# One decoder layer on one core: the first products' order, the norm of x on the way out of its transpose, eight early groups, and a ring of their own for gate rows

## The chip, the core and the metric

One NeuronCore of a Trainium2 chip runs the whole kernel. Its engines have a queue each: PE (TensorE, matrix products; its weight loads are shown as PEld), DVE (VectorE), ACT (ScalarE), POOL (GpSimd) and SP (SyncE, which here only issues DMAs). The metric is the device time of one execution in microseconds, and less is better. Of the kernel before there are three timed runs, and a trace of one more, profiled execution.

## The reference

```python
shift, scale, gate = split(silu(c) @ w_ada + b_ada, 3)
h = rms_norm(x, norm_pre_w) * (1 + scale) + shift
proj = h @ w_in        # q k v a b z of the delta net; qk v i f o z of the mLSTM; g_A g_B
y_A = (rms_norm(gated_delta_rule(...)) * silu(gdn_z)) @ w_proj_gdn
y_B = (sigmoid(ml_o) * rms_norm(mlstm(...)) * silu(ml_z)) @ w_proj_mlstm
out = (sigmoid(g_A) * y_A + sigmoid(g_B) * y_B) @ w_out
x + gate * rms_norm(out, norm_post_w)
```

x has 256 rows (SEQ) and 2048 columns (D), all in float32; c is one vector, so silu(c) @ w_ada is one row of 3 × 2048 numbers. The execution reads 354.40 MB from HBM, nearly all of it weights, each read once.

## The kernel before

**Products.** Each float32 operand is split in a high part (`whi`, `h_hi`; a cast on ACT, L169) and a remainder (`wlo`, `h_lo`; a subtraction on DVE or POOL, L170), and each product is made as three: hi·hi, hi·lo and lo·hi (`mm3`, L221 to L223). Weights come as units of up to 1 MB (`raw`, three buffers) that are used in pieces of 1024 columns; whi and wlo have four buffers each. `share` (L172) decides which remainders go to POOL instead of DVE: it counts up by 0.8 per column until POOL gets one, from a start of −3072.

**Order.** Nothing is scheduled by a compiler: each engine's queue holds instructions in the order in which the program writes them. `Stream` takes units; `_loads` issues a unit's DMAs on SP as soon as the unit that used its buffer before (one ring of buffers per name) is prepared in program order, and stops at the first unit for which that doesn't hold. `prep` (cast and remainder, or a sum) runs up to `ahead` pieces before `use` (the products). After each used piece `Side.step` lets every side generator go one `yield` further; norms, recurrences and gates are written as such generators, and `wait(n)` is n steps.

**Start.** silu(c) is spread over all partitions by products with one row (`csil`, L282). x is squared, and `rs` = 1/rms comes from DVE and POOL. `x_scale` (L300) multiplies x by rs on ACT, two chunks of 128 columns at a time; `x_turn` (L304) transposes them on PE, and ACT copies them back. Each row of w_ada (1 MB, `ar`, three buffers) is multiplied by csil and summed on DVE (L355); two rows give shift and scale of a chunk k of h. `h_chunk(k)` (L327) then makes sh, s1, hf, h_hi on ACT and h_lo on DVE for k < 2 and else on POOL. The 14 start groups are those columns of w_in that need h first: `BLOCKS` (L340) says which groups take which chunks in which order, and how many w_ada rows are loaded ahead. In block 0 the first `NE` = 6 groups take chunk 0, then the others chunks 0 and 1. Sums that aren't complete are kept in SBUF tiles `part` (L411 to L415).

**After the start** come eight periods of the delta net (`base_inverse`, L712, inverts triangles on DVE: `xx` goes to DRAM as `xd`, and comes back as `xcmp`, which DVE transposes into `ycmp` for PE), four mLSTM stages, in which 16 rows of w_ada for the gate are read as well (`add_gate_unit`, L1073, summed on DVE into `gacc`, L1089, and loaded into the ring of weights), and the output products.

Of the kernel before, what the change touches and what calls it, by code (L numbers as in the profile page):

```python
# [117 lines left out]
def hybrid_layer_kernel(  # L118
# [53 lines left out]
    share = [-3072.0, START_SHARE]  # L172
# [56 lines left out]
    ct = const("ct", c_t, [P, KC])  # L229
    sil = cp.tile([P, KC], F32, name="sil")  # L230
    A.activation(sil, ct, AF.Silu)
# [39 lines left out]
    crow = [part[4 + i].rearrange("p b c -> p (b c)")[0:1] for i in range(2)]  # L271
    for i in range(2):
        SP.dma_start(crow[i], c_row[:, i * 1024:(i + 1) * 1024])
    for b in range(2):
        SP.dma_start(xs[:, b], x[b * P:(b + 1) * P])
    SP.dma_start(ident, consts[:, 0:128])
    bat = const("bat", b_ada_t, [P, 32])
    npre = const("npre", npre_t, [P, KC])
    for i in range(2):
        A.activation(crow[i], crow[i], AF.Silu)  # L280
    for q in range(4):
        T.matmul(csil[:, q * 512:(q + 1) * 512], one_row, crow[q // 2][:, (q % 2) * 512:(q % 2 + 1) * 512],  # L282
                 start=True, stop=True)
    late_c = {}

    def late_consts():
        SP.dma_start(con[:, 128:512], consts[:, 128:512])
        late_c.update(gcv=const("gcv", gconv, [P, 256]), mcv=const("mcv", mconv, [P, 64]),
# [3 lines left out]
    for b in range(2):  # L292
        A.activation(part[2].rearrange("p b c -> p (b c)"), xs[:, b, 0:1024], AF.Square, accum_out=ss[:, b, 0:1])
        V.scalar_tensor_tensor(part[3].rearrange("p b c -> p (b c)"), xs[:, b, 1024:D], 1.0, xs[:, b, 1024:D],
                               op0=ALU.mult, op1=ALU.mult, accum_out=ss[:, b, 1:2])
    V.tensor_reduce(rs, ss, axis=AX.X, op=ALU.add)
    V.tensor_scalar(rs, rs, 1.0 / D, EPS, op0=ALU.mult, op1=ALU.add)
    pow_(rs, rs, mhalf[:, 0:2])

    def x_scale(k):  # L300
        for b in range(2):
            A.activation(xs[:, b, k * P:(k + 2) * P], xs[:, b, k * P:(k + 2) * P], AF.Copy, scale=rs[:, b:b + 1])

    def x_turn(k):  # L304
        ps = jtile("xps")
# [4 lines left out]
        A.copy(xs[:, :, k * P:(k + 2) * P], ps.rearrange("p (b c) -> p b c", b=2))  # L310


    for k in range(0, 8, 2):
        x_scale(k)
        if k in (2, 4):
            x_turn(k - 2)
# [3 lines left out]
    V.scalar_tensor_tensor(bnp, bat[:, KC:2 * KC], 1.0, npre, op0=ALU.add, op1=ALU.mult)  # L320

    def load_ada(src):
        raw = sp.tile([P, 2048], F32, name="ar", tag="ar", bufs=ADA_BUFS)
        SP.dma_start(raw, src)
        return raw

    def h_chunk(k):  # L327

        A.activation(sh[:, k:k + 1], ad[:, k:k + 1], AF.Identity, bias=bat[:, k:k + 1])
        A.activation(s1[:, k:k + 1], ad[:, KC + k:KC + k + 1], AF.Identity, bias=bnp[:, k:k + 1],  # L330
                     scale=npre[:, k:k + 1])
        hf = sp.tile([P, S], F32, name="hf", tag="hf", bufs=2)
        A.activation(hf.rearrange("p (b t) -> p b t", b=2), xs[:, :, k * P:(k + 1) * P], AF.Identity, bias=sh[:, k:k + 1], scale=s1[:, k:k + 1])
# [15 lines left out]
    def ada_units():  # L349

        adders = []
        for k in range(KC):
            for pt in range(2):
                def prep(h, raw, k=k, pt=pt):
                    V.scalar_tensor_tensor(raw, raw, 1.0, csil, op0=ALU.mult, op1=ALU.mult,  # L355
                                           accum_out=ad[:, pt * KC + k:pt * KC + k + 1])
                    j = 2 * (2 * k + pt) - 4
                    if 4 <= j < 16:
                        x_turn(j)
                        if j < 12:  # L360
                            x_scale(j + 4)
# [1044 lines left out]
```

## Time and profile before

| | |
|---|---|
| timed runs | 1602.19, 1605.75, 1607.46 us (median 1605.75) |
| the profiled execution | 1603.88 us, of it a span of 1601.9 us |
| mean granted clock | 0.999 |
| instructions | 25461 |
| DMA | 372.37 MB, 232 GB/s in the mean |

All times of the trace count from the start of the span. A matmul's duration overlaps the next one's, so the distance of two starts tells the rate. "Idle before" is the time that an engine did nothing ahead of an instruction, and the name behind the arrow is what ended it. The other lines of the profile stand where the prediction uses them.

### The profile page before, as it was taken

The page shows a single profiled execution, that of the slowest core. Times are in us where ns is not written, and L with a number is a line of the kernel's source. Part 1 is how long each engine was busy: PE and PEld are TensorE (multiplying, and loading weights), DVE is VectorE, ACT ScalarE, POOL GpSimd, SP SyncE. Part 2 cuts the span into 40 slices and gives each one's busy share as a digit, 9 for nine tenths or more (in the row PEclk, how much of TensorE's full clock was granted, in tenths as well). Part 3 has the DMA queues.
Part 4 walks back from the last instruction along what each step waited for, and adds up shares of the span by engine and source line. Part 5 has one row for each costly group of instructions (what it writes and reads, how often), then busy time and mean ns, then how long its engine had stood idle before and what let it go on. Part 6 is the DMA issues. An engine that isn't in the chain of part 4 may idle for free.

```text
span 1601.9 us, 25461 instructions
## 1 busy us (share of the span) xinstructions
PE 1577.8 (98%) x9844; PEld 1388.1 (87%) x9844; DVE 1150.1 (72%) x1801; ACT 941.0 (59%) x1503; POOL 236.7 (15%) x193
## 2 busy tenths in 40 slices
PE   7999999999999999999999999999999999999998
PEld 4888888899999999999999999889988888888886
DVE  6695556765689788887888788776878556756654
ACT  7754446765656575757576666655565644444443
POOL 1787771000000010000000000000000000100100
PEclk9999999999999999999999999999999999999999
DMA  9898775965565646564656465566888667766573
GB/s 375 339 406 335 279 274 195 289 238 191 170 203 175 205 148 204 164 193 169 193 169 195 149 197 176 187 214 247 290 308 305 227 249 284 283 246 244 200 273 113
DMA packets 96261, 372.37 MB, mean 232 GB/s; under 512 B 26262, under 2 KB 46214, under 8 KB 58252
## 3 DMA queue, kind: packets, MB, share of 16 engines
q1 hardware_dynamic: 96140, 370.75, 66.2%
q8 instruction: 77, 1.26, 0.3%
q14 instruction: 44, 0.36, 0.1%
HBM read 354.40 MB, written 16.31 MB: 231 GB/s over the span
## 4 chain that ended last, share of the span: by engine, by line
PE 79%; issue 13%; DMA 3%; DVE 2%; ACT 2%; POOL 1%; SPq 0%; DVEq 0%; POOLq 0%; ACTq 0%
PE pn L223 35%; PE pt L223 28%; PE py L223 8%; DMA raw<-in_dram 1%; POOL mg L1196 1%; PE psa L223 1%; ACT whi L169 1%; DVE wlo L170 1%; DMA ya<-o_dr 1%; DMA ar<-in_dram 1%; PE mz L816 0%; PE mq L807 0%; PE pa L828 0%; PE po L856 0%; PE po L857 0%
## 5 line engine op out<-in xcount | busy, mean ns | idle before, releaser
L170 DVE TENSOR_TENSOR wlo<-raw,whi 128x1024 fp32r<-128x1024 f32 x454 | 561.5, 1245 | 253.9 <-ACT whi L169 248.8
L169 ACT CAST whi<-raw 128x1024 fp32r<-128x1024 f32 (+1 forms) x517 | 533.0, 1046 | 327.1 <-PE pn L223 148.1
L223 PE MATMUL pt<-h_hi,whi 128*128 128x256 f32 x1280 | 367.8, 287 | 0.0
L223 PE MATMUL pt<-h_hi,wlo 128*128 128x256 f32 x1280 | 362.0, 283 | 0.0
L223 PE MATMUL pt<-h_lo,whi 128*128 128x256 f32 x1280 | 362.0, 283 | 0.0
L223 PE MATMUL pn<-whi,h_hi 128*128 128x512 f32 x896 | 353.9, 395 | 6.6 <-ACT whi L169 5.7
L223 PE MATMUL pn<-wlo,h_hi 128*128 128x512 f32 x896 | 350.0, 391 | 1.1 <-POOL wlo L170 0.6
L223 PE MATMUL pn<-whi,h_lo 128*128 128x512 f32 x896 | 349.8, 390 | 0.0
L223 PEld LDWEIGHTS pt<-h_hi,whi 128*128 128x128 f32 x1280 | 245.3, 192 | 1.4
L223 PEld LDWEIGHTS pt<-h_lo,whi 128*128 128x128 f32 x1280 | 245.4, 192 | 0.3
L223 PEld LDWEIGHTS pt<-h_hi,wlo 128*128 128x128 f32 x1280 | 245.2, 192 | 0.0
L223 PEld LDWEIGHTS pn<-whi,h_hi 128*128 128x128 f32 x896 | 168.8, 188 | 42.5 <-ACT whi L169 6.1
L223 PEld LDWEIGHTS pn<-wlo,h_hi 128*128 128x128 f32 x896 | 168.8, 188 | 36.0 <-DVE wlo L170 1.3
L223 PEld LDWEIGHTS pn<-whi,h_lo 128*128 128x128 f32 x896 | 168.6, 188 | 35.3
L170 POOL TENSOR_TENSOR wlo<-raw,whi 128x1024 fp32r<-128x1024 f32 (+1 forms) x63 | 146.3, 2332 | 67.1 <-ACT whi L169 64.9
L223 PE MATMUL py<-whi,yhi 128*128 128x512 f32 x384 | 150.6, 392 | 0.7 <-ACT vt L1017 0.7
L223 PE MATMUL py<-whi,ylo 128*128 128x512 f32 x384 | 149.6, 390 | 0.0
L223 PE MATMUL py<-wlo,yhi 128*128 128x512 f32 x384 | 149.4, 389 | 0.0
L411 DVE TENSOR_TENSOR part<-pn,part 128x512 f32<-128x512 f32 x112 | 73.7, 685 | 52.6 <-PE pn L223 52.6
L169 ACT CAST yhi<-ya 128x512 fp32r<-128x512 f32 x48 | 29.9, 622 | 130.9 <-PE py L223 127.4
L170 DVE TENSOR_TENSOR ylo<-ya,yhi 128x512 fp32r<-128x512 f32 x48 | 33.2, 692 | 86.7 <-ACT yhi L169 78.7
L593 DVE SCALAR_TENSOR_TENSOR qs<-pt,gcv,qs 128x255 f32<-128x255 f32 (+2 forms) x192 | 92.2, 480 | 4.6
(251 smaller groups left out, 1790.8 us busy)
## 6 DMA issues: line engine op xcount, KB each, us to landing
raw<-in_dram SPq DMA_DIRECT2D x259, 1024.0 KB
ar<-in_dram SPq DMA_DIRECT2D x32, 1024.0 KB
raw<-in_dram SPq DMA_DIRECT2D x16, 512.0 KB
ya<-o_dr SPq DMA_DIRECT2D x32, 256.0 KB
gate_dr<-part SPq DMA_DIRECT2D x11, 512.0 KB
gb<-rows SPq DMA_DIRECT2D x20, 256.0 KB
raw<-in_dram SPq DMA_DIRECT2D x6, 768.0 KB
ug<-ud SPq DMA_DIRECT2D x32, 128.0 KB
```

The lines of the kernel that those rows point to most:

```text
L169: A.copy(hi, src)
L170: (eng or V).tensor_tensor(lo, src, hi.bitcast(F32), op=ALU.subtract)
L223: T.matmul(ps, l, r, start=start and i == 0, stop=stop and i == 2, skip_group_check=True)
L411: V.tensor_tensor(part[g][:, b], ps[b], part[g][:, b], op=ALU.add)
L593: V.scalar_tensor_tensor(dst[:, n, sh:], src[:, 0:S - sh], taps(n, 3 - sh), dst[:, n, sh:], op0=ALU.mult, op1=ALU.add)
L1196: G.tensor_tensor(mcols(b, hf, cg), mcols(b, hf, cg), s_, op=ALU.add)
```

## The change

At the start the row of c is loaded by ACT's queue, w_ada's first row ahead of x by SP's, its second in two halves, and three small constants by POOL's; silu(c) by partitions is made later. A tile of zeros is multiplied with itself four times (`keep_busy`) after csil, and once more behind the first transposes. Squares, rs, the two sums, the first cast (now on DVE) and the first chunk are written out in one function, `first_chunk`, which scales only the first two chunks of x; hf is read from PSUM. The first twelve products go by part over four banks (`use_first`). For the other chunks raw x is transposed, and DVE multiplies it with `rsb`, rows of rs, on the way out of PSUM (`x_norm`). rsb comes from two POOL operations and two products with the identity, written after the eighth group of block 0 (`rs_rows`). sh and s1 of the other chunks are DVE's; h_lo is DVE's for chunks 1 and 15, else POOL's. Eight groups are early instead of six, and share starts at −1024. In the periods of the delta net a step is moved ahead of `block_rows` and into `base_inverse`, and xd's store, its reload and the transpose are two steps apart each. A gate row is loaded as four tiles of 512 columns, in a ring of one row.

```diff
-    share = [-3072.0, START_SHARE]
+    share = [-1024.0, START_SHARE]
+    begin = []
...
+        if begin:
+            begin.pop()(raw[:, 0:n], hi, lo)
+            return hi, lo
...
+    crow = ada_tile()[0:1]
+    A.dma_start(crow, c_row)
+    ar0, ar1 = load_ada(w_ada[0]), ada_tile()
     for b in range(2):
         SP.dma_start(xs[:, b], x[b * P:(b + 1) * P])
...
+    for t, src in ((bat, b_ada_t), (npre, npre_t), (ident, consts[:, 0:128])):
+        G.dma_start(t, src)
     for i in range(2):
+        SP.dma_start(ar1[:, i * 1024:(i + 1) * 1024], w_ada[1][:, i * 1024:(i + 1) * 1024])
...
+    zero = part[-1][:, 0]
+    G.memset(zero, 0.0)
+    zps = jtile("zps")
+    def keep_busy(n):
+        for _ in range(n):
+            T.matmul(zps, zero[:, 0:P], zero, start=True, stop=True)
...
+    def x_norm(k):
+        ps = x_turn(k)
+        V.tensor_tensor(xs[:, :, k * P:(k + 2) * P].rearrange("p b (k t) -> p b k t", k=2), ps,
+                        rsb.rearrange("p (b t) -> p b t", b=2).unsqueeze(2).broadcast_to([P, 2, 2, P]), op=ALU.mult)
+    def rs_rows():
+        ps = jtile("rsp")
+        for b in range(2):
+            rc = part[-1][:, 1, b * P:(b + 1) * P]
+            G.tensor_scalar(rc, zero[:, 0:P], rs[:, b:b + 1], None, op0=ALU.add)
+            T.matmul(ps[:, b * P:(b + 1) * P], rc, ident, start=True, stop=True)
+        A.copy(rsb, ps[:, 0:S])
...
+    def first_chunk(src, hi, lo):
+        keep_busy(4)
+        half = [slice(i * 1024, (i + 1) * 1024) for i in range(2)]
...
+        G.tensor_tensor(rs, ss[:, :, 0], ss[:, :, 1], op=ALU.add)
+        G.tensor_scalar(rs, rs, 1.0 / D, EPS, op0=ALU.mult, op1=ALU.add)
+        pow_(rs, rs, mhalf[:, 0:2])
+        ada_sum(ar0, slice(0, D), ad[:, 0:1])
+        V.scalar_tensor_tensor(bnp, bat[:, KC:2 * KC], 1.0, npre, op0=ALU.add, op1=ALU.mult)
+        for i in range(2):
+            ada_sum(ar1, half[i], adh[:, i:i + 1])
...
+        A.activation(sh[:, 0:1], ad[:, 0:1], AF.Identity, bias=bat[:, 0:1])
+        V.tensor_copy(hi, src)
+        for b in range(2):
+            A.activation(xs[:, b, 0:2 * P], xs[:, b, 0:2 * P], AF.Copy, scale=rs[:, b:b + 1])
+        xps = x_turn(0)
+        keep_busy(1)
+        V.tensor_tensor(lo, src, hi.bitcast(F32), op=ALU.subtract)
+        hf = sp.tile([P, S], F32, name="hf", tag="hf", bufs=2)
+        A.activation(hf.rearrange("p (b t) -> p b t", b=2), xps[:, :, 0], AF.Identity, bias=sh[:, 0:1],
+                     scale=s1[:, 0:1])
+        split(hf, h_hi[:, 0], h_lo[:, 0], V)
...
-        split(hf, h_hi[:, k], h_lo[:, k], V if k < 2 else G)
+        split(hf, h_hi[:, k], h_lo[:, k], V if k in (1, KC - 1) else G)
...
-    NG, NE = len(START), 6
+    NG, NE = len(START), 8
...
-    BLOCKS = ((EARLY, 0, 1, 1.1, 3.5), (REST, 0, 2, 4, 8), (EARLY, 1, 3, 8, 12), (REST, 2, 2, 12, 16.5),
+    BLOCKS = ((EARLY, 0, 1, 1.1, 2.8), (REST, 0, 2, 4, 8), (EARLY, 1, 3, 8, 13), (REST, 2, 2, 13, 16.5),
...
+                    if pt:
+                        V.scalar_tensor_tensor(s1[:, k:k + 1], ad[:, KC + k:KC + k + 1], npre[:, k:k + 1],
+                                               bnp[:, k:k + 1], op0=ALU.mult, op1=ALU.add)
+                    else:
+                        V.tensor_tensor(sh[:, k:k + 1], ad[:, k:k + 1], bat[:, k:k + 1], op=ALU.add)
+                    if 2 <= k < 9 and pt == 0:
+                        x_norm(2 * k - 2)
...
+        def use_first(hi, lo):
+            pss = [[jtile(f"pn{i}") for i in range(2)] for _ in range(2)]
+            for i, (l, r) in enumerate(((h_hi, hi), (h_hi, lo), (h_lo, hi))):
+                for g in range(2):
+                    for b in range(2):
+                        T.matmul(pss[g][b], l[:, 0, b * P:(b + 1) * P], r[:, g * 512:(g + 1) * 512],
+                                 start=i == 0, stop=i == 2, skip_group_check=True)
...
+                stream.ahead = 3 if bi else 2
+                if bi == 0 and g == 0:
+                    use_first(hi, lo)
+                    return
...
+                    if bi == 0 and gg == NE - 1:
+                        rs_rows()
-                stream.ahead = 3 if bi else 1
...
-        yield from wait(4)
+        yield from wait(3)
...
-        yield from wait(1)
+        yield from wait(2)
         SP.dma_start(xd.rearrange("qq q rg m i -> (q rg m) qq i"), xx)
+        yield from wait(2)
...
-        yield from wait(5)
+        yield from wait(2)
...
+        raw = [yp.tile([P, 512], F32, name=f"graw{q}", tag=("yhi", "ylo")[q % 2], bufs=2) for q in range(4)]
+        for q in range(4):
+            SP.dma_start(raw[q], src[:, q * 512:(q + 1) * 512])
...
-        stream.add(w_ada[32 + i], prep, None, 1)
+        stream.add(w_ada[32 + i], prep, None, 1, load=(load_gate, "gate", 1))
```

What this does to the queues, as the two programs write them (line, operation, out and in by their names, size, and how many in a row). PE from its first product of csil up to the first products of w_in, before:

```order
L282 MATMUL csil<-part_110,one_row 128x512 x2
L282 MATMUL csil<-part_111,one_row 128x512 x2
L308 MATMUL xps<-con,xs 128x128 x8
L223 MATMUL pn_221<-whi,h_hi 128x512
L223 MATMUL pn_221<-wlo,h_hi 128x512
L223 MATMUL pn_221<-whi,h_lo 128x512
L223 MATMUL pn_222<-whi,h_hi 128x512
```

and the same place of PE's queue after the change (zps is the bank of the zeros, part_117 the tile that holds them, con the constants with the identity):

```order
L297 MATMUL csil<-ar,one_row 128x512 x4
L305 MATMUL zps<-part_117 128x512 x4
L329 MATMUL xps<-con,xs 128x128 x4
L305 MATMUL zps<-part_117 128x512
L476 MATMUL pn_212<-whi,h_hi 128x512
L476 MATMUL pn_213<-whi,h_hi 128x512
L476 MATMUL pn_214<-whi,h_hi 128x512
L476 MATMUL pn_215<-whi,h_hi 128x512
L476 MATMUL pn_212<-wlo,h_hi 128x512
```

Five products of zeros stand around the first transposes, of which there are four instead of eight, and the first four products need whi and h_hi alone.

POOL's queue from the loads of the small constants to the first of its remainders, after the change (rsx is rs, ssx the sums of squares; before, the queue had only the power and then remainders):

```order
L291 DMA bat<-in_dram 128x32
L291 DMA npre<-in_dram 128x16
L291 DMA con<-in_dram 128x128
L299 MEMSET part_117 128x512
L369 TENSOR_TENSOR rsx<-ssx 128x2
L370 TENSOR_SCALAR rsx<-rsx 128x2
L223 TENSOR_TENSOR rsx<-rsx,mhalf 128x2
L170 TENSOR_TENSOR wlo<-raw,whi 128x1024 x3
L344 TENSOR_SCALAR part_117<-part_117,rsx 128x128 x2
L170 TENSOR_TENSOR wlo<-raw,whi 128x1024
```

The two operations for rows of rs stand behind three remainders on POOL, and the products that read them stand on PE behind the 48th product of w_in.

SP's queue around the last store of xd, which falls into the first mLSTM stage, before:

```order
L164 DMA raw<-in_dram 128x2048 x7
L745 DMA xd<-xx 128x8x32
L748 DMA xcmp<-xd 32x1x256 x4
L164 DMA raw<-in_dram 128x2048 x5
L901 DMA o_dr<-oT 128x2x256 x2
```

and after (graw are the tiles of the gate rows):

```order
L164 DMA raw<-in_dram 128x2048 x2
L824 DMA xd<-xx 128x8x32
L828 DMA xcmp<-xd 32x1x256 x4
L1157 DMA graw_11234<-in_dram 128x512
L1157 DMA graw_11235<-in_dram 128x512
L1157 DMA graw_11236<-in_dram 128x512
L1157 DMA graw_11237<-in_dram 128x512
L164 DMA raw<-in_dram 128x2048
L981 DMA o_dr<-oT 128x2x256 x2
```

Gate rows are no longer among the raw loads, and four DMAs stand in SP's queue for one of them.

More of the change, by code (lines that the diff above doesn't have):

```diff
@@ L290, in late_consts @@
                       gnw=const("gnw", gnorm, [P, 1]), mnw=const("mnw", mnorm_t, [P, KC]))
[L292 to L302, printed above, removed]
+    rsb = con[:, 128:384]
     def x_turn(k):
@@ L309, in x_turn @@
                             ident)
[L310 to L316, printed above, removed]
-    bnp = sp.tile([P, KC], F32, name="bnp")
[L320 to L325, printed above, removed]
+        return ps.rearrange("p (b k t) -> p b k t", b=2, k=2)
@@ L351, in ada_units @@
         adders = []
-        for k in range(KC):
+        for k in range(1, KC):
             for pt in range(2):
@@ L541, in hybrid_layer_kernel @@
             ahead = first + (last - first) * j / len(fs)
-            while ia < len(ada) and ia < ahead:
-                ada[ia]()
+            while ia - 2 < len(ada) and ia < ahead:
+                ada[ia - 2]()
                 ia += 1
@@ L694, in gdn_stage1 @@
                 scored[0] = p
+        yield
         block_rows(res, z)
-        yield
         for blk in range(2):
@@ L712, in base_inverse @@
     def base_inverse(zg, res, zr):
+        yield
         ud = res["ud"]
```

79 lines of the change are left out of this document (49 added, 30 removed).

## The prediction

> **What bounds the kernel now.** First the page's totals, then busy time cut into stages by the windows view (columns: busy us and count of each engine, granted clock, DMA share, GB/s).
>
> ```profile
> PE 1577.8 (98%) x9844; PEld 1388.1 (87%) x9844; DVE 1150.1 (72%) x1801; ACT 941.0 (59%) x1503; POOL 236.7 (15%) x193
> ...
> 0.00:20.00 20.00, 9.16 (x16) 3.82 (x16) 8.27 (x18) 12.74 (x24) 0.92 (x5) 1.00 0.86 338
> 20.00:86.00 66.00, 64.00 (x278) 50.95 (x279) 48.33 (x48) 51.76 (x90) 39.58 (x22) 1.00 0.94 368
> 86.00:257.00 171.00, 171.00 (x756) 141.57 (x755) 109.91 (x126) 78.33 (x96) 115.88 (x55) 1.00 0.83 310
> ...
> 1063.00:1100.00 37.00, 34.60 (x319) 31.37 (x318) 24.78 (x40) 21.81 (x43) 1.85 (x1) 1.00 0.70 256
> ...
> 1585.00:1602.00 17.00, 9.24 (x41) 7.32 (x39) 6.39 (x11) 2.76 (x6) 3.68 (x4) 0.90 0.34 123
> ```
>
> TensorE is the bound: 1577.8 of 1601.9 us, 24.1 us idle. So the change can win only in the idle time and in the slow matmuls of the start: 10.8 us before the first product at 20.00, 2.0 us up to 86, 2.4 us at 1063 to 1100, and 7.8 us at the end, which it doesn't touch. From 86 to 1063 nearly every microsecond is PE's, so what is won at 86 is kept, and what isn't won by 86 is lost.
>
> Then the timeline of the start (start, duration, engine, line; in brackets what ended the idle time).
>
> ```profile
> 1.82 0.83 SPq L275 DMA_DIRECT2D xs<-in_dram  x2
> ...
> 3.88 7.19 PE L282 MATMUL csil<-part,one_row 1*128 1x512 f32 x8 [3.88 <-ACT part L280]
> 6.68 1.06 ACT L293 ACTIVATE part<-xs 128x1024 f32<-128x1024 f32 x1 [1.91 <-DMA xs<-in_dram]
> 9.26 1.06 ACT L293 ACTIVATE part<-xs 128x1024 f32<-128x1024 f32 x1 [1.43 <-DMA xs<-in_dram]
> 11.06 0.71 POOL L219 TENSOR_TENSOR rsx<-rsx,mhalf 128x2 f32<-128x2 f32 x1 [10.62 <-DVE bnp L320]
> ...
> 15.22 2.29 DVE L355 SCALAR_TENSOR_TENSOR ar<-ar,csil 128x2048 f32<-128x2048 f32 x1
> 17.55 0.39 ACT L330 ACTIVATE s<-ad,bnp,npre 128x1 f32<-128x1 f32 x1 [1.12 <-DVE ar L355]
> 17.97 0.60 ACT L333 ACTIVATE hf<-xs,sh,s 128x256 f32<-128x256 f32 x1
> 18.60 0.40 ACT L169 CAST h_hi<-hf 128x256 fp32r<-128x256 f32 x1
> 18.91 1.99 ACT L169 CAST whi<-raw 128x1024 fp32r<-128x1024 f32 x2
> 20.00 0.80 PE L223 MATMUL pn<-whi,h_hi 128*128 128x512 f32 x1 [5.67 <-ACT whi L169]
> 21.27 0.79 PE L223 MATMUL pn<-wlo,h_hi 128*128 128x512 f32 x1 [0.47 <-DVE wlo L170]
> ...
> 22.29 0.63 PE L223 MATMUL pn<-whi,h_hi 128*128 128x512 f32 x1
> ...
> 24.42 0.63 PE L223 MATMUL pn<-whi,h_lo 128*128 128x512 f32 x1
> ...
> 25.59 0.39 PE L223 MATMUL pn<-whi,h_hi 128*128 128x512 f32 x1
> ...
> 29.44 0.39 PE L223 MATMUL pn<-whi,h_lo 128*128 128x512 f32 x1
> ...
> 34.12 1.04 PE L308 MATMUL xps<-con,xs 128*128 128x128 f32 x8
> ...
> 36.02 0.50 PE L223 MATMUL pn<-wlo,h_hi 128*128 128x512 f32 x1 [0.63 <-POOL wlo L170]
> ```
>
> Read backwards, the chain is: w_ada's second row summed (15.22), scale, `hf`, `h_hi`, the weight's cast, the first product. From 22.29 to 24.42 five products start 0.427 us apart, from 25.59 to 29.44 seventeen 0.226 apart. So the array is at half rate for 4.8 us after 20.00, although the clock column says 1.00.
>
> **The change, part by part.**
>
> *Loads.* Today x is issued at 1.82 and its first half used at 6.68: 4.86 later; the second follows 2.58 later. With ar0 first on SP (at about 0.7), I estimate ar0 at 5.5, x at 8.2 and 10.8, ar1's halves at 12.1 and 13.4: the second w_ada row 1.8 earlier than 15.22, now half at a time.
>
> *csil* keeps its 7.19 us and ends near 10.6, so DVE sums ar0 from 10.6 to 12.9, `bnp`, and then two halves of about 1.2 each; s1 is there at about 16.0.
>
> *The norm* has three squares on ACT after 8.2: 10.8 + 2 × 1.2 = 13.2. Then POOL's add, scale and pow: an add on POOL takes 0.35 by the row below, pow 0.71, so about 14.7; two ACT scales (0.46 each, L302) give 15.6.
>
> *The zeros.* One fp32 product of 512 columns takes 7.19 / 4 = 1.80 us in csil's row, or 0.95 at the fast rate (by 0.226 / 0.427). Four take 3.8 to 7.2 us; I take 5.7, half slow and half fast: 10.6 to 16.3. The transposes wait behind them on PE (0.6 us for four), then `hf` 0.60, `h_hi` 0.40: first product at **18.05** instead of 20.00. The fifth, 0.95, runs beside `hf`; slow, it would cost 0.7. The weight's cast moves from ACT to DVE behind s1 (about 1.2, by 1.22 of DVE's row of this size below; done near 17.2), the remainder takes 1.22 more, so wlo (18.4) and h_lo (18.9) come before products 5 and 9 want them (19.0, 19.9): the order by part is what hides them. If the zeros worked, twelve products take 12 × 0.227 = 2.7, done at 20.8 instead of 25.59: **4.8 us**.
>
> ```profile
> L640 POOL TENSOR_TENSOR b<-gb,ngt 128x2 f32<-128x2 f32 x16 | 5.7, 354 | 0.0
> L302 ACT ACTIVATE xs<-xs,rsx 128x256 f32<-128x256 f32 x16 | 7.3, 516 | 1.4 <-POOL rsx L219 1.4
> ...
> L411 DVE TENSOR_TENSOR part<-pn,part 128x512 f32<-128x512 f32 x112 | 73.7, 685 | 52.6 <-PE pn L223 52.6
> L170 POOL TENSOR_TENSOR wlo<-raw,whi 128x1024 fp32r<-128x1024 f32 x58 | 139.7, 2415 | 66.5 <-ACT whi L169 64.3 <-PE pn L223 2.2
> ```
>
> The array's rate is where a rule can be held against a row. csil kept PE busy for 7.19 us with one-row operands and the transposes after 12.37 and the products from 20.00 still ran slow. The Trainium skill, "TensorE: Matmul & The Clock Gate", Part 1, says that about 3.4 us of sustained work opens the clock and an idle window of that length closes it again, by how busy the array is. By that rule the zeros open it, and the fifth one after the transposes keeps it open, which is the sum above; by csil's row they may not, which is rival A. No run here shows full-height zeros.
>
> *What takes part of it back.* Eight groups first means 48 products before the next chunk: 18.05 + 48 × 0.227 = 28.9, while DMA is full (0.94 of the window 20 to 86 already). Loads start only 1.1 us earlier than now, so PE will catch up with them, and with four banks copied out at once: I give 1 to 2 us (bounds 0 and 4.8, all of it). Then two new matmuls (`rsp`) on PE wait for two POOL operations that stand behind POOL's wlo pieces, 2.4 us each. I estimate them at 31.3 to 32.6, when PE could have been there at 29.5 to 30.5: about 2 us of stall. The 49th product comes at 32.5 to 33.8 (today after the transposes of 34.12, at 34.91).
>
> *x's new way out* spares ACT two scales (1.03) and a copy per pair of chunks and gives DVE one operation from PSUM (near L411's 0.69), and sh and s1 too. ACT and DVE have 14 and 18 us to spare in the window 20 to 86, so this is worth nothing directly. One more set of four transposes falls behind the first product: 0.5 (half of 34.12's 1.04). Against that, stalls such as the 0.63 at 36.02 mostly go, POOL starting earlier and more groups being open: 1.5 of the 2.0 idle us. At 86 I count 1.8 + 1.5 − 0.5 = **2.8 us** gained (0.3 to 5.5).
>
> *GDN waits and gate rows.* At 1063 to 1100:
>
> ```profile
> PE mp L781 <- DVE ycmp L752: 1.9, 1, 1.9
> ...
> PE pab L223 <- POOL h_lo L170: 0.4, 1, 0.4
> ...
> SPq L164 <- DVE gacc L1089: 34.1, 15, 4.2
> SPq L748 <- DMA xd<-xx: 24.1, 8, 6.2
> 1065.75 1.29 DVE gacc L1089
> 1067.05 5.00 DMA raw<-in_dram
> ...
> 1072.13 1.06 ACT whi L169
> ...
> 1073.22 1.22 DVE wlo L170
> ...
> 1087.45 8.72 DMA raw<-in_dram
> ```
>
> The first rows are waits (total, count, longest), the last five the chain of waits: a gate row in the weights' ring is read by DVE, only then the next weight is loaded, and ACT's cast waits for it; DVE's order, with the transpose PE waits for, slips with it. With rings apart, weights go out earlier; I take **2.0** of the 2.4 idle us (0 to 2.4). Four DMAs per gate row take SP about 1.7 us for 0.4 (0.83 for two of x), and DVE two more, shorter instructions; PE's products cover both. The last chunk's h_lo on DVE removes pab's **0.4**. In the GDN periods xd's store and its reload are now two steps apart, and two more follow before the transpose, six in all as before: SP is no longer held while xd is written (24.1 us in eight periods, 3.0 each, 6.2 at worst). A step is a piece of twelve products, 2.7 us, so the reload has about 5.4 us against a round of 3.0. I count nothing; if it came late, mp's 1.9 would stand in seven more periods, 13 us. PE without a gap there today gains nothing from it.
>
> **Sum**: 2.8 + 2.0 + 0.4 = 5.2 us. The profiled execution took 1603.88 (span 1601.9), which gives 1598.7; the median of the runs is 1605.75, 1.9 more, and on that I predict **1600.5**, with 1597.5 to 1603 if the mechanism holds.
>
> **Rivals.**
>
> A. *The zeros don't open the clock* (for: csil's row; against: those used one row of the array, these 128). Four slow ones end at 17.8, the first product is at 19.5 to 20.3, slow, and the dozen ends near 25: nothing before 86 but one removed stall against added transposes. The other 2.4 stand: 1603.3. Chance 0.16.
>
> B. *The supply takes it*: they open it, but weights and `rsp` cost nearly all the 4.8 (for: DMA at 0.94 over 20 to 86; against: seventeen products without a gap from 25.59). 0.5 + 2.4 = 2.9: 1602.8. Chance 0.16.
>
> C. *More than forecast*: `rsp` arrives in time and the removed stalls count whole: 5.5 + 2.4 = 7.9: 1597.8. Chance 0.16.
>
> D. *Slower*: a ring of one for gate rows. The four pieces of gate row i+1 wait on SP until DVE has read row i, and every weight load behind them waits too, while the old ring let two others pass. Today a row's wait is 4.2 at worst, and the latest landing 8.72 us. A load of weights lasts 24 products, 5.5 us, and four buffers let a cast run three pieces, 8.2 us, ahead, of which it and the remainder take 2.3: once row and load together need more than about 11 us, PE waits the rest for each. Three late by 3 us, with 1063's 2.0 not won, cost 9 − 3.2 = 5.8: 1611.5. Against: 2 MB at the 256 GB/s of that window are 8.2 us. Chance 0.08.
>
> **How the numbers follow.** Forecast 0.44. A measurement here tells 0.3% (4.8 us) from no change, so faster begins at 1600.9. Of the forecast some six tenths lie below (0.27), C whole (0.16), A and B 0.03: faster 0.46. Slower is D: 0.08. The rest is 0.46. The range reaches from below C, 1594.5, to 1607, beyond A and B and short of D.
>
> **What would show it.** Zeros: first products 0.227 apart, near 18; at 0.427 it is A. The twelfth done near 20.8; the 49th near 33; a wait of PE on POOL's `part` ahead of `rsp` (about 2 us; none means C; a wait on raw before it means B). The gain at 86 is read from when the 254th product on PE starts. No wait of `mp` on `ycmp`, none of `pab` on h_lo; if casts wait on raw behind `graw` loads it is D. I am wrong if idle time turns up between 86 and 1063, where I count none.

## The result and the profile after

The changed kernel is slower: 1627.01 us median (1626.66 to 1627.57) against 1606.17 (1602.19 to 1607.46), a ratio of 1.0131 with a 95% interval of 1.0116 to 1.0146. The forecast was 1600.5 with a range to 1607. The profiled execution took 1627.23 us with a span of 1625.5, 23.6 more than the span before. The kernel before was timed anew beside each group of runs, with medians from 1604.25 to 1606.17, so kernels of different groups are compared by their ratios to it.

The page's first lines of the changed kernel, and its busy time by the stages that the prediction used:

```profile
PE 1591.7 (98%) x9858; PEld 1390.9 (86%) x9858; DVE 1183.9 (73%) x1873; ACT 921.2 (57%) x1452; POOL 246.9 (15%) x202
```

```profile
0.00:20.00 20.00, 16.04 (x29) 6.90 (x30) 9.39 (x20) 10.38 (x17) 3.71 (x11) 1.00 0.92 343
20.00:86.00 66.00, 60.44 (x268) 47.26 (x267) 57.35 (x64) 39.62 (x61) 41.04 (x25) 1.00 0.94 365
86.00:257.00 171.00, 165.73 (x722) 136.30 (x721) 122.84 (x139) 71.00 (x79) 118.58 (x56) 0.98 0.79 299
...
310.00:1063.00 753.00, 747.52 (x5728) 689.80 (x5727) 586.52 (x1138) 479.39 (x811) 45.77 (x75) 1.00 0.56 187
```

The last of these stretches, which the prediction doesn't show, before:

```profile
310.00:1063.00 753.00, 753.00 (x5784) 698.70 (x5783) 598.34 (x1156) 481.83 (x830) 44.87 (x76) 1.00 0.57 187
```

PE is still 98% busy, and 13.9 us busier than before; 7.1 of that are the zeros, and some is the same work at half rate, so busy time alone doesn't show the loss. The windows do: PE, without a gap from 86 to 257 before, has 5.3 us of them there now, and at a granted clock of 0.98; 753.00 of 753.00 became 747.52; and 20 to 86 lost 3.6 us of busy time where it should have won.

The sharper reading is by position: how early or late the same product starts. All the kernels here have the same 8112 products with a weight on PE, so the start of the n-th one can be compared. In microseconds, counted in the traces' PE rows (the first column of numbers is the time before, the others the difference to it; the columns e1 to e3 belong to the first experiments below):

| n-th product | before | after | e1 (sh, s1 on ACT) | e2 (old steps) | e3 (gates in raw ring) |
|---|---|---|---|---|---|
| 1 | 20.00 | −1.53 | −0.86 | −0.28 | −1.86 |
| 13 | 25.59 | −4.08 | −3.41 | −2.83 | −4.39 |
| 49 | 34.91 | +0.06 | +0.13 | +2.39 | −0.98 |
| 254 | 85.99 | +1.09 | −0.74 | +2.38 | +0.51 |
| 317 | 100.31 | +10.46 | +1.33 | +11.93 | +9.84 |
| 1061 | 264.83 | +9.77 | +1.00 | +11.21 | +9.13 |
| 5701 | 1072.14 | +20.09 | +10.70 | +11.22 | +20.19 |
| 5841 | 1099.77 | +17.20 | +7.82 | +8.34 | +17.31 |
| 6341 | 1193.20 | +18.81 | +9.12 | +10.20 | +17.31 |
| 6591 | 1240.03 | +23.26 | +11.83 | +15.68 | +17.75 |
| 8112 | 1593.86 | +23.26 | +11.80 | +16.00 | +17.75 |

So the start won 4.1 us by the 13th product, and all of it was gone at the 49th. Then 9.4 us went between the 254th and the 317th, 10.3 in the delta net's periods, 1.6 in the mLSTM stages, and 4.5 just ahead of the first output products; 2.9 came back at 1072 to 1100. The positions are of one execution each. Kernels with the same start (the changed one, e2, e3, e4) have their first product anywhere from 17.60 to 19.73, and the traced execution of e1, 1615.78 us, is 4.0 below the median of its runs, so a difference of a microsecond or two tells nothing.

The start on PE in the changed kernel's timeline:

```profile
10.81 6.09 PE L305 MATMUL zps<-part 128*128 128x512 f32 x8
...
18.47 1.20 PE L476 MATMUL pn<-whi,h_hi 128*128 128x512 f32 x4 [0.28 <-ACT h_hi L169]
19.51 1.08 PE L476 MATMUL pn<-wlo,h_hi 128*128 128x512 f32 x4
20.43 1.08 PE L476 MATMUL pn<-whi,h_lo 128*128 128x512 f32 x4
...
28.72 0.50 PE L227 MATMUL pn<-whi,h_hi 128*128 128x512 f32 x1 [0.76 <-ACT part L486]
...
31.30 0.50 PE L227 MATMUL pn<-whi,h_hi 128*128 128x512 f32 x1 [1.62 <-DVE part L488]
```

Twelve products in 3.0 us and a first one at 18.47 are near the forecast 2.7 and 18.05. Then PE waits for banks that ACT and DVE have still to copy out.

The timeline around 90 us, where the first large loss is, on DVE, POOL and PE:

```profile
85.51 4.77 POOL L170 TENSOR_TENSOR wlo<-raw,whi 128x1024 fp32r<-128x1024 f32 x2 [1.90 <-ACT whi L169]
...
88.62 1.67 DVE L420 SCALAR_TENSOR_TENSOR s<-ad,npre,bnp 128x1 f32<-128x1 f32 x1
90.22 2.27 DVE L417 SCALAR_TENSOR_TENSOR ar<-ar,csil 128x2048 f32<-128x2048 f32 x1
...
92.39 4.67 POOL L170 TENSOR_TENSOR wlo<-raw,whi 128x1024 fp32r<-128x1024 f32 x2 [0.22 <-ACT whi L169]
...
92.53 2.22 DVE L423 TENSOR_TENSOR sh<-ad,bat 128x1 f32<-128x1 f32 x1
94.68 0.68 DVE L336 TENSOR_TENSOR xs<-xps,con 128x512 f32<-128x512 f32 x1
...
95.41 0.79 PE L227 MATMUL pn<-whi,h_hi 128*128 128x512 f32 x1 [4.50 <-DVE xs L336]
```

Two DVE operations on one element per partition take 1.67 and 2.22 us. The first ends at 90.29, as POOL's pair of remainders does (85.51 + 4.77 = 90.28). The second starts 0.14 after POOL's next remainder and ends at 94.75; those two remainders take 4.67, so the first of them ends near 94.74. The same holds for all 27 of these 30 operations that start while POOL works: each ends within 0.02 us of a POOL instruction's end. The three that meet no work of POOL take 0.16, 0.16 and 0.22. Behind them in DVE's queue is the multiplication that frees the transposes' bank, PE waits 4.50 for that bank, and then its products are at half rate: the row of 95.41 has 0.79 us where others have 0.39.

The waits in the later stages, from the view of waits (total, count, longest), of which the first stood at none and the second at 2.0 us before, and the third, SP's, at 34.1 (for the rows in the ring of weights):

```profile
ACT x L835 <- DMA xcmp<-xd: 20.6, 12, 3.4
...
DVE nsu L804 <- DMA ug<-ud: 19.4, 6, 4.2
...
SPq L1157 <- DVE gacc L1179: 71.4, 46, 10.8
```

The second of them before:

```profile
DVE nsu L725 <- DMA ug<-ud: 2.0, 2, 1.2
```

### The profile page after: what moved, and what is told of

Its sections match the earlier page's. It is cut to its first block, busy times and chain, and to the rows that moved or that the text cites. A ratio compares the mean times of both kernels' runs of the same rounds, so it can differ in the third digit from the quotient of the medians.

```text
span 1625.5 us, 25583 instructions
## 1 busy us (share of the span) xinstructions
PE 1591.7 (98%) x9858; PEld 1390.9 (86%) x9858; DVE 1183.9 (73%) x1873; ACT 921.2 (57%) x1452; POOL 246.9 (15%) x202
## 4 chain that ended last, share of the span: by engine, by line
PE 62%; issue 14%; DVE 11%; DMA 6%; ACT 4%; POOL 1%; SPq 1%; DVEq 0%; ACTq 0%; POOLq 0%
PE pn L227 28%; PE pt L227 20%; PE py L227 8%; DVE wlo L170 4%; ACT whi L169 1%; DMA xd<-xx 1%; DMA ug<-ud 1%; DVE ar L417 1%; DVE qs L671 1%; DVE tmp L815 1%; DMA xcmp<-xd 1%; POOL mg L1285 1%; DMA ya<-o_dr 1%; DMA gb<-rows 1%; DVE xx L819 1%
```

## The experiments

**e1 and e4: where sh and s1 are made.** e1 takes them back to ACT in `h_chunk`; e4 leaves them on DVE but gives each a single tensor input and takes the rest from pointers to scalars.

```diff
# e4
-                        V.scalar_tensor_tensor(s1[...], ad[...], npre[:, k:k + 1], bnp[:, k:k + 1], op0=ALU.mult, op1=ALU.add)
+                        V.tensor_scalar(s1[...], ad[...], npre[:, k:k + 1], bnp[:, k:k + 1], op0=ALU.mult, op1=ALU.add)
...
-                        V.tensor_tensor(sh[...], ad[...], bat[:, k:k + 1], op=ALU.add)
+                        V.tensor_scalar(sh[...], ad[...], bat[:, k:k + 1], None, op0=ALU.add)
```

> The changed kernel with sh and s1 of chunks 1 to 15 back on ACT; nothing else is undone. Theory 1: these two tiny DVE operations wait for the POOL remainder that runs beside them (1.67 us for s and 2.22 us for sh at 88.6 and 92.5, both ending with POOL's instruction), so DVE's release of the transposes' bank comes late and PE stands 4.50 us ahead of 95.41 and then runs at half rate. Then the wait is gone, and the 8.9 us that the changed kernel loses between its 260th and 283rd weight product are won back: 1627.0 minus 8 to 11, 1616 to 1619. Theory 2: DVE is late for the sum of its work (two sums of 2.28, the norm of x on the way out), and the tiny operations only add their 0.2 each: then less than 2 us come back, 1625 to 1627.

> The changed kernel with sh and s1 still on DVE, made by an operation with one tensor input and pointers to per-partition scalars instead of two tensor inputs. Theory 1a: only a DVE instruction with two SBUF tensor inputs waits for POOL's: each takes some 0.2 us even where POOL's remainder runs, the wait at 95 is gone, time as with both on ACT within 1 us, 1616 to 1619. Theory 1b: any DVE instruction of this size waits, and durations stay at 0.6 to 2.2 us and the time at 1625 to 1628. Theory 2 (sum of DVE's work): 1625 to 1627 with short durations.

e1: 1619.82 us, ratio to the kernel before 1.0090 (1.0066 to 1.0114). e4: 1618.04, 1.0085 (1.0060 to 1.0109). Theory 1 gave 1616 to 1619, theory 2 1625 to 1627, so e4 is as expected and e1 0.8 beside it; in the table e1 stands at +1.33 at the 317th product instead of +10.46; e4 at +2.31. The groups of the two operations, in the changed kernel and in e4 (busy us, mean ns of one):

```profile
L420 DVE SCALAR_TENSOR_TENSOR s<-ad,npre,bnp 128x1 f32<-128x1 f32 x15 | 16.1, 1076 | 0.5
L423 DVE TENSOR_TENSOR sh<-ad,bat 128x1 f32<-128x1 f32 x15 | 12.8, 853 | 0.5
```

```profile
L420 DVE TENSOR_SCALAR s<-ad,npre,bnp 128x1 f32<-128x1 f32 x15 | 4.1, 273 | 0.6
L423 DVE TENSOR_SCALAR sh<-ad,bat 128x1 f32<-128x1 f32 x15 | 3.2, 214 | 0.5
```

The same engine, the same place in its queue, the same numbers computed: with two tensor inputs 0.85 and 1.08 us in the mean, with one 0.21 and 0.27, although POOL's remainders run beside them as before. That leaves theory 1a. The sum of DVE's work (theory 2) can't explain durations. Nor are the two-input forms slow in themselves, by the three of 0.16 to 0.22 us above.

**e2 and b1: the steps.** e2 puts the old steps into the changed kernel, b1 the new steps alone into the kernel before.

```diff
# b1
+        yield
         block_rows(res, z)
-        yield
...
+        yield
...
-        yield from wait(4)
+        yield from wait(3)
...
-        yield from wait(1)
+        yield from wait(2)
         SP.dma_start(xd...., xx)
+        yield from wait(2)
...
-        yield from wait(5)
+        yield from wait(2)
```

> The changed kernel with the steps of the delta net's periods as before (block rows one step earlier, four steps from the loads of ug, one ahead of xd's store, the reload at once, five ahead of the transpose). Theory: two steps are too few for the reload of xcmp, ACT's copies of it wait (12 waits, 20.6 us, none before), casts of weights queue behind them, and likewise DVE for ug (19.4 us, 2.0 before); undone, the 9.5 us lost between 265 and 1066 come back: 1616 to 1619, with no waits of ACT on xcmp. Rival: the loss there comes from the gate rows or from the later order of DVE alone, and the steps are innocent: 1625 to 1628.

> The kernel before with the changed steps in the delta net's periods alone. Theory: the loss of 9.4 us up to 1066 belongs to the steps alone, whatever the start: 1605.6 plus 8 to 10, 1613.6 to 1616, with waits of ACT on xcmp and of DVE on ug. Rival: it takes the later start or the gate rows as well: below 1610.

e2: 1618.04 us, ratio 1.0079 (1.0060 to 1.0099). From the 1061st to the 5701st product it stays at +11.2: the whole loss of the periods is gone, and with it the waits of ACT on xcmp and of DVE on ug. b1: 1613.39, ratio 1.0050 (1.0037 to 1.0063); it is 0.40 ahead of the kernel before at the 1061st product and 10.1 behind at the 5701st, with this wait:

```profile
ACT x L757 <- DMA xcmp<-xd: 16.0, 7, 3.1
```

b1's time is 0.2 us below what was expected, the mechanism as expected: it needs neither the new start nor the gate rows. In the changed kernel one such place reads like this, on SP and ACT:

```profile
756.55 1.99 ACT L169 CAST whi<-raw 128x1024 fp32r<-128x1024 f32 x2
756.67 2.76 SPq L828 DMA_DIRECT2D xcmp<-xd  x4
...
761.00 0.41 ACT L835 COPY x<-xcmp 32x256 f32<-32x256 f32 x1 [2.45 <-DMA xcmp<-xd]
...
761.82 1.26 ACT L835 COPY x<-xcmp 32x256 f32<-32x256 f32 x3 [0.41 <-DMA xcmp<-xd]
...
763.10 1.05 ACT L169 CAST whi<-raw 128x1024 fp32r<-128x1024 f32 x1
```

The reload is issued at 756.67 and the first of its four pieces is there at 761.0, 4.3 us later. Two steps are 5.4 us of PE's time, as the prediction has it, but in ACT's queue only two casts stand there, done in 1.99 us, so ACT asks for xcmp (the start of its copy less the idle time before it) 1.9 us after the issue. Over the eight periods of the changed kernel ACT asks for it from 0.4 us before the issue to 1.9 after it; in the kernel before it was 4.8 to 9.8 after it. ACT stands still for 2.45 and 0.41 us, and the weights' cast, which has nothing to do with xcmp, stands behind the copies in ACT's queue and comes at 763.10; the casts are late from there on, and at 771.69 PE waits 0.76 us for a remainder.

No run parts this wait from DVE's on ug, which the same steps bring (24.1 us in b1). By position 7.8 of the 10.3 us are lost within 25 us behind a wait of ACT on xcmp, and the last 2.3 at 1060 to 1067, behind DVE's wait of 4.22 for ug at 1048.94; DVE's seven earlier waits for ug have no loss in the 40 us behind them.

**e3: gate rows in the ring of weights again.**

```diff
-        stream.add(w_ada[32 + i], prep, None, 1, load=(load_gate, "gate", 1))
+        stream.add(w_ada[32 + i], prep, None, 1)
```

> The changed kernel with gate rows loaded into the ring of weights again, as whole rows, and two DVE instructions per row. Theory: the ring of its own won the 2 us near 1066 (20.1 behind there, 17.2 after it) and lost them again up to the first output products, where four DMAs per row stand in SP's queue behind the DVE's reading (waits of SP on gacc 80.7 us instead of 36.3) and a cast waits 2.33 at 1256.65: within 2 us of 1627.0. Rival: the loads held by it cost more than it wins: 1622 to 1624.

1622.03 us, ratio 1.0104 (1.0085 to 1.0122): 5.0 below the changed kernel, more than the 2 us of the theory, so the rival is the better one. The table places it: e3 goes through the stretch ahead of the first output products, where the changed kernel loses 4.5 us between the 6341st and the 6591st product, with 0.4, and through the mLSTM stages between the 5841st and the 6341st with none of the 1.6. The four traces with the ring of their own (the changed kernel, e1, e2, e4) lose 1.3 to 1.9 us in those stages and 2.7 to 5.5 ahead of the output products; all others lose none in the first and −0.4 to 2.6 in the second, the 2.6 in b1, where PE waits 2.83 us for another operation of ACT (`vt`).

The 2.9 us at 1072 to 1100 are won by e3 too, although its gate rows are in the ring of weights. That stretch takes 24.75 us, with no wait of `mp` on `ycmp`, in every kernel with the new steps (b1 and e3 among them, with the old ring) and in e2, with the old steps and the new ring; in the kernels with neither it takes 25.5 to 29.2. Either of the two is enough.

The place ahead of the output products in the changed kernel:

```profile
1241.70 2.73 DVE L1179 SCALAR_TENSOR_TENSOR gacc<-graw,sil,gacc 128x512 f32<-128x512 f32 x4
...
1242.47 2.91 SPq L1157 DMA_DIRECT2D graw<-in_dram  x4
...
1245.90 0.42 SPq L1222 DMA_DIRECT2D ya<-o_dr  x1
...
1255.04 0.62 ACT L169 CAST yhi<-ya 128x512 fp32r<-128x512 f32 x1 [6.95 <-DMA ya<-o_dr]
```

```profile
1256.65 0.50 PE L227 MATMUL py<-whi,yhi 128*128 128x512 f32 x1 [2.33 <-ACT whi L169]
```

The four DMAs of a gate row wait on SP for DVE's reading of the row before (L1179, 2.73 us); what stands behind them, the first load of y for the output products, goes out at 1245.90, and ACT's cast waits for it until 1255.04. In e3 it goes out at 1243.08 and the cast starts at 1249.83.

**c1: all three undone; b2: the two operations alone.** c1 holds the edits of e1, e2 and e3; b2 puts sh and s1 with two inputs into the kernel before.

> The changed kernel with sh and s1 on ACT, the old steps of the delta net's periods and gate rows in the ring of weights, all three. Theory: the three losses lie in different stages and add (8.9 near 95, 9.4 up to 1066, 5 around 1250, all by the 23.3 that the changed kernel is behind at the last weight product): 1627.0 minus 22 to 25, 1602 to 1606, on par with the kernel before, its lead of the start lost by the 48th product as in the single steps. Rival: one of the losses is replaced by the next wait: 1608 to 1614.

> The kernel before with sh and s1 on DVE, with two tensor inputs, alone. Theory 1: each waits for the POOL remainder beside it, 0.8 to 1.1 us in the mean as in the changed kernel, some 25 us of DVE in all; ACT still takes the transposes out of PSUM here, so PE is not held by it directly, and the loss is smaller than 8.9: plus 0 to 5, 1605 to 1611. Theory 2 (sum of DVE's work): durations near 0.2, time within 1 us of 1605.6.

c1: 1606.67 us, ratio 1.0006 (0.9996 to 1.0015), 0.7 above the range of its theory. The three losses add (by the ratios 0.41, 0.52 and 0.27% of the 1.31), and without them the rest of the change makes no difference that these runs can tell. b2: 1608.11, ratio 1.0022 (1.0010 to 1.0033), with means of 896 and 597 ns: the wait is there without the rest of the change, and costs less. That ACT still frees the transposes' banks there was the reason expected; what the trace shows is one wait of PE of 3.29 us at 87.61, for sums on DVE that stand behind an s of 1.34.

**Where the start's 4 us go.** Five more kernels, all on c1's ground or on the kernel before. c3: sh and s1 with one input on DVE, and the rows of rs made right behind the power. d1: as c1, rows of rs early, and the copies of the first six groups on ACT. d2: c1 without zeros. d3: c1 with six early groups and the old table of blocks. d4: the kernel before with four products of zeros.

```diff
# c3, d1
         pow_(rs, rs, mhalf[:, 0:2])
+        for b in range(2):
+            G.tensor_scalar(part[-1][:, 1, b * P:(b + 1) * P], zero[:, 0:P], rs[:, b:b + 1], None, op0=ALU.add)
# d1
-                elif bi or b == 0 or g % 2 == 0:
+                elif bi or g < 6 or b == 0:
# d4, behind the first transposes
+    zero = part[-1][:, 0]
+    G.memset(zero, 0.0)
+    zps = jtile("zps")
+    for _ in range(4):
+        T.matmul(zps, zero[:, 0:P], zero, start=True, stop=True)
```

> As the run with three undone, but sh and s1 on DVE with one tensor input, and the two POOL operations that make rows of rs issued right behind the power instead of behind three remainders. Theory: PE's wait for them (1.8 and 2.1 us in the runs with sh and s1 mended) goes, so the 49th product comes 2 us earlier than there, near 33, and what the start wins is kept: 1599 to 1603. Rival: the supply of weights takes the place of that wait, 49th near 34.5, and the time is that of the other within 1 us.

> As the run with three undone, with the rows of rs made early on POOL, and the copies of the banks of the first six groups of block 0 on ACT, as in the kernel before, instead of every fourth on DVE. Theory: the lead of 3.5 us at the 12th product is lost up to the 48th because a copy on DVE stands behind a sum of w_ada (2.28 us) that itself waits for its load, and PE waits for the bank (2.73 at 30.59, then 3.4 us at half rate): with ACT the wait is at most 0.8, the 49th product comes 2 to 4 us earlier than in the run with three undone (37.3), at 33.5 to 35, and the time is 1601 to 1604. Rival: the weights' supply (ACT's casts wait for loads there) gives the same 49th product within 1 us: 1605 to 1608.

> The run with three undone, without the five products of zeros. Theory: the zeros open the clock (first products 0.227 apart with them), so without them the first products are 0.427 apart for some 4 us and the 12th comes 2 to 3 us later than 22.1, at 24 to 25.5; since the lead is lost by the 48th anyway, the time is within 2 us of 1606.7. Rival: the row of csil's products would have opened it, 12th within 0.5 us of 22.1.

> The run with three undone, with six early groups and the old table of blocks. Theory: with six groups 36 products stand before the second chunk instead of 48, rows of rs and the second chunk are wanted earlier, and PE waits there 1 to 3 us more: 1607 to 1611. Rival: the two more groups only load DMA at the time it is full, and six are better by 1 to 3 us: 1603 to 1606.

> The kernel before with four products of zeros on PE behind the first transposes, nothing else. Theory: the clock is open at the first product (20.0), the first twelve come 0.227 apart except where they wait for wlo, the 12th 2 to 3.5 us earlier than 25.59, and of it 0 to 1.5 us are left after the 48th, since loads are full: 1603 to 1605.6. Rival: all of it is kept: 1601 to 1602.5.

| run | us | ratio to before (95%) | 1st product | 13th | 49th | 85th | 317th |
|---|---|---|---|---|---|---|---|
| before | | | 20.00 | 25.59 | 34.91 | 44.95 | 100.31 |
| c1 | 1606.67 | 1.0006 (0.9996 to 1.0015) | −0.90 | −3.47 | +2.43 | +2.98 | +3.75 |
| c3 | 1606.85 | 1.0016 (1.0005 to 1.0026) | −0.39 | −2.94 | +0.96 | +4.55 | +7.42 |
| d1 | 1609.49 | 1.0030 (1.0018 to 1.0042) | −1.35 | −3.91 | −2.23 | +2.32 | +3.09 |
| d2 | 1609.10 | 1.0020 (1.0011 to 1.0030) | −2.31 | −3.36 | −0.58 | −0.01 | +0.77 |
| d3 | 1607.18 | 1.0013 (1.0004 to 1.0022) | −1.49 | −2.62 | +0.87 | −0.55 | +2.28 |
| d4 | 1603.34 | 0.9986 (0.9977 to 0.9994) | −0.35 | −0.72 | −0.39 | −0.41 | −0.42 |

The traced executions are no median ones: c3's is 5.9 us above the median of its runs and c1's 2.6 above, d1's 4.1 and d2's 3.9 below. c3 and d1 both fail to keep the lead. In d1 the 49th product comes 2.2 us early, as its theory has it, but at the 85th it is nearly as far behind as c1, waiting for DVE (2.08 us for the multiplication at 43.70), and its time is no better. In c3 the wait for the rows of rs is gone, as meant, but waits of 2.21 for a bank and 1.76 for a remainder stand in its place.

d2 misses: without zeros the 13th product comes as early as with them, since the transposes don't stand behind the zeros. The first product is at 17.70, and the slow rate then costs what the zeros cost. Its time is 2.4 us above c1's, with intervals of the ratios that overlap, so what the zeros are worth in the whole stays open. d3 lies at the lower edge of its theory's range and 0.5 us from c1, which tells nothing.

d4 is the only one that wins, 0.14%: less at the 13th product than expected, since the profiled execution had gone back to half rate (a granted clock of 0.79 in the window 20 to 28), and the time as expected. Its trace is only 0.45 us ahead of the one before at the last product, so the positions don't show where the rest of the 0.14% comes from.

The last two tell the loads from DVE's queue. f1 loads eight rows of w_ada by half and has DVE sum that half twice; f2 loads them whole and has DVE sum one half once; both leave the other half out of these sums. f3 adds h_lo of the last chunk on DVE to d4.

```diff
# f1
+        SP.dma_start(raw[:, 0:1024], src[:, 0:1024])
...
+                    if k < 5:
+                        V.scalar_tensor_tensor(raw[:, 0:1024], raw[:, 0:1024], 1.0, csil[:, 0:1024], ..., accum_out=adh[:, 0:1])
+                        V.scalar_tensor_tensor(raw[:, 0:1024], raw[:, 0:1024], 1.0, csil[:, 0:1024], ..., accum_out=ad[...])
# f3
-        split(hf, h_hi[:, k], h_lo[:, k], V if k < 2 else G)
+        split(hf, h_hi[:, k], h_lo[:, k], V if k < 2 or k == KC - 1 else G)
```

> The run with the copies on ACT, with eight rows of w_ada (chunks 1 to 4) loaded by half, 4 MB less in all; DVE sums the loaded half twice, so its work stays (the other half of these sums is left out). Theory S (supply): DMA is full from 4 to 52 us (414 GB/s, 1.02 of its share from 20 to 44), and each kernel has its 84th product where the loads ahead of it have landed; 4 MB at 414 GB/s are 9.7 us, of which the 84th can gain what it stands behind PE's own time, 4 to 7: it comes at 40 to 43 instead of 47.3, and the time is 3 to 7 us below 1609.5. Theory Q (DVE's queue of sums, 2.28 each, ahead of what PE waits for): 84th within 1.5 us of 47.3, time within 2 us.

> The same kernel with all loads whole, but DVE summing only one half of these eight rows, once (1.25 instead of 2.28 each; the other half is left out). Theory S: 84th product within 1.5 us of 47.3. Theory Q: it comes 2 to 6 us earlier.

> The kernel before with the four products of zeros, and h_lo of the last chunk on DVE instead of POOL. PE's wait of 0.4 on it goes: 0 to 0.5 us below the run with the zeros alone, 1602.8 to 1603.3; if DVE's order costs as much elsewhere, no difference.

f1: 1605.08 us (ratio 1.0001, 0.9992 to 1.0010); its 85th product comes at 44.79, 2.5 us ahead of d1's 47.27. f2: 1604.51 (1.0001, 0.9991 to 1.0010); at 43.47, 3.8 ahead. From 20 to 44 us the windows of d1, f1 and f2 are:

```profile
20.00:44.00 24.00, 19.24 (x84) 14.20 (x83) 18.95 (x19) 20.12 (x35) 13.54 (x7) 0.99 1.02 414
```

```profile
20.00:44.00 24.00, 20.38 (x90) 15.28 (x89) 18.70 (x28) 20.20 (x36) 12.33 (x6) 1.00 0.88 312
```

```profile
20.00:44.00 24.00, 22.20 (x95) 17.45 (x94) 12.48 (x18) 20.38 (x36) 11.81 (x6) 0.93 1.02 411
```

In f1 DMA is no longer full (0.88) and PE wins only 1.1 us of busy time; in f2 DVE's busy time falls from 18.95 to 12.48 us while DMA stays full, and PE wins 3.0. f2 is what theory Q says. f1 fits neither whole: at 2.5 us it gains less than S's 4 to 7 and more than Q's 1.5 by position, while its time, 4.4 below d1's, is in S's range. So both hold the start: DVE's queue, with the sums, a copy, a multiplication and remainders in order, and the loads. By position the first is the larger part, and f2's trace has 3.4 us of half rate (29.79 to 33.20) that f1's doesn't have; but that is one trace of each, and in time both are worth the same: the ratio falls from d1's 1.0030 to 1.0001. Neither keeps the lead whole. How the two share it isn't settled.

f3: 1603.11 us, ratio 0.9988 (0.9979 to 0.9997). Like d4 it beats the kernel before, by some 2 us; the 0.2 between f3 and d4 is inside what the runs scatter.

## Why the prediction was wrong, point by point

- **The first products**: right. 18.47 for 18.05, the 13th product 4.1 us early for 4.8. The zeros' 5.7 us were 6.09 (half slow and half fast is 5.5 by the prediction's own terms, and its sum to 18.05 comes to 17.9). But the zeros, on which the 4.8 was built, weren't what won it, and in that the number was luck: in d2, without them, the 13th product is as early, so they cost the transposes what they gave the products. What won it is the rest of the new start, the order by part and the earlier sums, which no run parts.
- **"What takes part of it back"**: under-sized. I gave 1 to 2 us for supply and bank copies and 2 for the rows of rs, with the 49th product at 32.5 to 33.8; it came at 34.97. The wait for the rows of rs was sized well where it shows (1.77 us in e1, 2.10 in e4; in the changed kernel PE comes too late to wait more than 0.1). The rest was 4.1 us: the 48th product starts at 33.25, and from 18.47 without a wait it would have been 29.1.
- **"ACT and DVE have 14 and 18 us to spare in the window 20 to 86, so this is worth nothing directly"**: this is the step that failed first. It priced the moved operations by the engines' idle time, not by what stands behind them. sh and s1 took 28.9 us on DVE (16.1 + 12.8), where by their size they take 7.3 (e4), and the multiplication that frees PE's bank stands behind them. e1: 9.1 us by position at the 317th product, and 7.2 in time (e4: 9.0). The prediction weighed a rule on the clock and not the one that spoke against this step: the Trainium skill, "SBUF — State Buffer", says under "SBUF: two separate sides" that a DVE operation with two SBUF inputs and a GpSimd operation that reads SBUF take a shared pair of ports in turn, the second waiting for the whole instruction of the first. By that rule I estimate that each of the two waits up to a remainder's 2.4 us, some 1.2 on average where POOL is busy; the trace has 0.85 and 1.08, and agrees.
- **"I count nothing; if it came late, mp's 1.9 would stand in seven more periods, 13 us"**: the failing case, with the right price: 10.3 us in the changed kernel and b1's 10.5. The step that failed is the 5.4 us for the reload. It counted two steps in PE's time; ACT, which copies xcmp, has two casts there and asks after 1.9 us at most, while the reload takes 4.3 from issue to landing. The round of 3.0 set against it came from the wrong row too, SP's wait on xd's store, which ends when the store does. And what waited was ACT with a weight's cast behind it, not only PE on `ycmp`. That ACT's wait is the larger cause and DVE's on ug the smaller is read from positions; no run parts them.
- **Gate rows, "I take 2.0 of the 2.4 idle us"**: 2.9 us came at 1072 to 1100, and `mp` waits no more. The ring does that (e2), but it isn't needed: the new steps, counted at nothing, do the same without it (b1, e3). What the ring cost is rival D on a smaller scale and at other places: 1.6 us in the mLSTM stages, by a wait whose cause stays open, and up to 4.5 where y's loads stand behind the gate row's four DMAs; 5.0 in time by e3. "PE's products cover both" didn't hold there, and the four DMAs took SP 2.91 us at 1242.47 where 1.7 were estimated.
- **pab's 0.4**: right, the wait is gone, and between the 317th and the 1061st product the difference falls by 0.7 (by 0.34 in f3; in d4, without this, by nothing).
- **"I am wrong if idle time turns up between 86 and 1063, where I count none"** named the place: 19.0 of the 23.3 us went between the 254th and the 5701st product. A stage in which PE is busy all the time has no reserve to win, but everything to lose: each move of work there should have been priced from below.

## What to carry to other kernels

A tiny operation isn't free because it is tiny: before it moves to another engine, read what runs beside it there, how many tensor inputs it has, and what stands behind it in that queue. Where several steps of waiting are dealt out again, each piece must still cover the transfer that it hides, from issue to landing, counted in the queue of the engine that will ask for it, and a late transfer costs the engine that waits for it, with all that is queued there. And a lead at the start is worth nothing until what follows (loads, sums, copies of banks) can keep its pace.

## What the runs showed of the hardware

- A DVE instruction with two SBUF tensor inputs, one element per partition, that starts while POOL runs an instruction with two tensor inputs of 1024 columns ends when POOL's does, 27 times of 27 in the changed kernel: 1.67 us at 88.62 and 2.22 at 92.53. With one tensor input and pointers to scalars it takes 0.21 to 0.28 us in the same place (e4). Where POOL stood idle, the two-input forms took 0.22 and 0.16 (102.58, 37.12).
- Products with one row of weights (csil) keep PE busy for 7.19 us without raising its rate: their eight instructions stay 0.85 us apart. Right behind them in the changed kernel, zeros of full height go from 0.85 to 0.43 apart, 4.8 us after their start (eight in 6.09 us). In d4 eight take 4.08, the rate rising 1.0 us after the first; there transposes stand ahead of them. The Trainium skill, "TensorE: Matmul & The Clock Gate", Part 1, says that the clock is set by how busy PE has been recently; the trace agrees only if one row of it doesn't count as busy.
- A wait of PE of 4.5 us costs more than itself: after 4.50 us ahead of 95.41 the granted clock is 0.50 from 94.16 to 100.99, and the difference to before grows from +6.2 at the 268th product to +8.9 at the 283rd with no further wait. Shorter waits did it in some traces (3.4 us of half rate around the end of waits of 2.73 in c1 and 1.80 in f2) and not in others (2.83 in b1 at 1247.46, 1.90 before at 1080.83). The kernel before has no wait above 1.9 us behind the first product.
